# A two-layer transformer block on one core: FFN gate and up products by Strassen's scheme for 18 of 22 feature tiles

## The chip, the cores and the metric

The kernel runs on one core of a Trainium2 chip. The metric is the device time of one execution in microseconds (us). The kernel before the change takes 1743.31 us, the median of 3 runs (1742.58 to 1743.42).

The engines are TensorE (PE; PEld is its weight load), VectorE (DVE), ScalarE (ACT), GpSimd (POOL) and SyncE (SP), which issues every DMA of this kernel. Matrix products are written to PSUM, in banks of 128 x 512 fp32; everything else lies in SBUF. DVE and ACT can read PSUM, POOL works on SBUF only.

## The reference, cut to what matters

```
for l in range(2):
    h = rms_norm(x, g_pre_mix[l])
    mix = hybrid_mixer(h, ...)                      # four attention branches, gates, w_out
    x = x + rms_norm(mix, g_post_mix[l])
    h = rms_norm(x, g_pre_ffn[l])
    f = (silu(h @ w_ffn_gate[l]) * (h @ w_ffn_up[l])) @ w_ffn_down[l]
    x = x + rms_norm(f, g_post_ffn[l])
```

There are 512 tokens, the model is 1024 wide (8 tiles of 128) and the FFN 2816 wide (22 tiles of 128, `FT`). All of it is float32.

## The kernel before, in words

**Three products for one.** A product of float32 matrices is made of three fp32r products. Each operand x is split into hi, a rounded copy made by ACT, and lo = x - hi, made by DVE or POOL. `mm3` (L304) issues hi·hi, hi·lo and lo·hi into one PSUM bank (L306, L307, L308); the lo·lo product is left out. Each of the three has a weight load of its own.

**Layout.** In the FFN, features lie on the partitions and the 512 tokens on the free axis. `u` holds the 8 split tiles of the FFN's input, times its gain but not yet times the rms factor of each token. That factor, broadcast over the partitions, is `rB`.

**Weights.** `plan()` (L58) lists all weight tiles in the order in which they are used; the host lays them out in that order. `w_load` (L231) has SP load a tile of 128 x 1024 (512 KB) into one of three `raw` buffers. `conversion` (L249) splits it into `whi` and `wlo` (four buffers each) in two halves of 512 columns: an ACT cast (L271) and a DVE subtraction (L272) for each half. `take` (L280) hands the next tile out and converts two tiles ahead (`CL`).

**The FFN.** `ffn` (L1385) goes over the 22 feature tiles. `fm` (L772) takes a weight tile and issues 8 x 3 products of 512 columns into a PSUM bank, once for gate and once for up. DVE multiplies the gate product by `rB` (L1390), ACT applies silu (L1391), POOL multiplies by `rB` again (L1392), which stands for the factor of the up product, DVE multiplies by the up product (L1409), and ACT and POOL split the result into hi and lo (L298, L299) for the down product. The first five of the 44 products are issued at the end of `out_block` (L1252), which hands them over as `ps`.

**What follows.** In layer 0, `down_block` (L1162) takes one column of 128 features after the other over 22 feature tiles. In layer 1, `finish` (L1428) has tokens on the partitions and weights 256 columns wide as the moving operand (`tm`, L792 to L794). Both read the residual only near their ends: `x` in layer 0, and in layer 1 `xt`, which `to_tokens` (L1415) makes of `x` by transposes during the FFN.

**Order.** Tile assigns the order of instructions on each engine when the program is built, by dependencies and program order, except between `ordered(True)` and `ordered(False)`, where the order is as written. Each engine then runs its own queue in that order. `act` is a pool of 63 buffers of 128 x 512 (`AB`), tag `a`; `hp` has 12 more for the hidden tiles.

Of the kernel before, what the change touches and what calls it, by code (L numbers as in the profile page):

```python
# [17 lines left out]
S = 512  # L18
# [28 lines left out]

G0, G1, S1, TS, GT = 2, 4, 4, 5, 3
SQ = 3
LAST_K = ((0, 2), (2, 2), (4, 2), (6, 2), (8, 4), (12, 4), (16, 4), (20, 2))  # L50


def _ktiles(w, k0, nk, cols):
    w = w[k0 * 128:(k0 + nk) * 128][:, cols]
    return w.reshape(nk, 128, -1).transpose(1, 0, 2)


def plan():  # L58

    out = []  # L60

    def add(name, nk, nc, f):
        out.append((name, nk, nc, f))

    for l in range(LAYERS):
        def w_in(name, k0, nk, cols):
            add(name, nk, len(cols), lambda a, l=l: _ktiles(a["w_in"][l], k0, nk, cols))

        def rng(key, n, o=0):
            return np.arange(OFF[key] + o, OFF[key] + o + n)  # L70
# [22 lines left out]
        for m in range(FT):  # L93
            for key in ("w_ffn_gate", "w_ffn_up"):
                add(key, 8, 128, lambda a, l=l, m=m, key=key:
                    _ktiles(a[key][l], 0, 8, np.arange(m * 128, m * 128 + 128)))
        if l < LAYERS - 1:
            for d in range(8):
                for k0, nk in ((0, 8), (8, 8), (16, 6)):
                    add("down", nk, 128, lambda a, l=l, d=d, k0=k0, nk=nk:  # L100
                        _ktiles(a["w_ffn_down"][l], k0, nk, np.arange(d * 128, d * 128 + 128)))
        else:
            for c in range(4):
                for k0, nk in ((0, 4), (4, 4), (8, 4), (12, 4), (16, 4), (20, 2)) if c < 3 else LAST_K:
                    add("held" if c == 3 and nk == 2 and k0 < 8 else "downt", nk, 256, lambda a, l=l, c=c, k0=k0, nk=nk:
                        _ktiles(a["w_ffn_down"][l], k0, nk, np.arange(c * 256, c * 256 + 256)))
    return out


# [84 lines left out]
class Builder:  # L194
# [28 lines left out]
    def stream_init(self):  # L223
        self.wi = 0
        self.n_dma = self.n_conv = 0
        self.woff = [0]
        for _, nk, nc, _ in self.plan:
            self.woff.append(self.woff[-1] + 128 * nk * nc)
        self.raw, self.whl = {}, {}

    def w_load(self, upto):  # L231
        while self.n_dma <= min(upto, len(self.plan) - 1):
            i = self.n_dma
            _, nk, nc, _ = self.plan[i]
            n = nk * nc

            t = self.a() if i < 2 else self.wraw.tile([128, 1024], F32, tag="raw", name="raw")
            self.nc.sync.dma_start(
                t[:, :n], self.ap["wts"][self.woff[i]:self.woff[i + 1]].rearrange("(p n) -> p n", p=128))
            self.raw[i] = t  # L240
            self.n_dma += 1

    def w_conv(self, upto):

        while self.n_conv <= min(upto, len(self.plan) - 1):
            for f in self.conversion():
                f()

    def conversion(self, lo_engine=None):  # L249
# [5 lines left out]
        t = self.raw.pop(i)  # L255
        kh = (nk + 1) // 2
        if name == "held":
            tiles = [(self.ar(), self.ar()) for _ in range(2 if nk * ncol > 512 else 1)]
            if len(tiles) == 1:
                kh = nk  # L260
# [19 lines left out]
    def take(self, name, ahead=None):  # L280
        i = self.wi
        assert self.plan[i][0] == name, (self.plan[i][0], name)
        self.w_conv(i + (CL if ahead is None else ahead))
        self.wi += 1
        return self.whl.pop(i)


    def split(self, src, scale=None, lo_engine=None):
# [59 lines left out]
                                  start=True, stop=True)  # L348
        return ss

    def rms(self, ss, nt=4):

        r, steps = self.rms_steps(ss, nt)
        for _ in steps:
            pass
        return r

    def rms_steps(self, ss, nt=4):
        v, r, t = (self.small(nt) for _ in range(3))

        def steps():
            self.nc.vector.tensor_scalar(v, ss[:, 0:nt], 1.0 / D, RMS_EPS, op0=ALU.mult, op1=ALU.add)
            yield
            yield from self.root(v, r, t)
        return r, steps()

# [478 lines left out]
        return acc[0]  # L845

    def next_factors(self, ss):
        self.rT = self.rms(ss)

    def next_spread(self):  # L850
        ps = self.spread(self.rT)
# [310 lines left out]
    def down_block(self, xs, gain, x, next_gain):  # L1162
# [28 lines left out]

        def sums(half):
            ss[half] = self.token_sums(acc, None, 2 * half, 2)
            r[half], chain[half] = self.rms_steps(ss[half], 2)

        def start(half):
            rb[half] = self.spread(r[half], 2)[:, 0:256]
# [184 lines left out]
        self.ordered(False)  # L1382
        return u, y, out

    def ffn(self, l, u, ps):  # L1385
        nc = self.nc
        hid = []

        def silu(z, s, ps, rb):
            nc.vector.tensor_mul(z, ps, rb)  # L1390
            nc.scalar.activation(s, z, AF.Silu)  # L1391
            nc.gpsimd.tensor_mul(s, s, rb)  # L1392

        def keep(s):
            if len(hid) >= FT - 6:
                pr = tuple(self.hp.tile([128, 512], F32R, tag="h", name="h") for _ in range(2))
            else:
                pr = self.ar(), self.ar()
            hid.append(pr)
            return pr  # L1400

        for m in range(FT):
            gate = ps.pop(0) if ps else (yield from self.fm("w_ffn_gate", u))
            z, s = self.a(), self.a()
            silu(z, s, gate, self.rB)
# [3 lines left out]
            nc.vector.tensor_mul(s, s, up)  # L1409
            pr = keep(s)  # L1410
            self.split_to(pr[0], pr[1], s, lo_engine=nc.gpsimd)
            yield 3
        return hid

    def to_tokens(self, x, xt):  # L1415
        nc = self.nc
# [11 lines left out]
    def finish(self, hid, xt):  # L1428
# [8 lines left out]
        for c in range(4):  # L1437
            def evac(t, ps, c=c):
# [6 lines left out]
                if c == 2:  # L1445
                    s1 = before[:, t:t + 1]
                    nc.vector.tensor_reduce(s1, ss[:, 4 * t:4 * t + 3], axis=mybir.AxisListType.X, op=ALU.add)
                    nc.vector.tensor_scalar(s1, s1, 1.0 / D, RMS_EPS, op0=ALU.mult, op1=ALU.add)
# [36 lines left out]
    def build(self):  # L1485
        nc, tc = self.nc, self.tc
        with ExitStack() as ctx:
# [6 lines left out]
            self.ct = cp.tile([128, NCON], F32, name="ct")  # L1494
            self.vt = cp.tile([128, NVEC], F32, name="vt")
            self.gnh = cp.tile([128, 4], F32, name="gnh")
            self.stream_init()
            nc.sync.dma_start(self.vt, self.ap["vec"])
            x = []
# [11 lines left out]
            for l in range(LAYERS):  # L1511
                last = l == LAYERS - 1
                with tc.tile_pool(name="pt%d" % l, bufs=2) as self.ptp:
# [10 lines left out]
                with tc.tile_pool(name="hid%d" % l, bufs=12) as self.hp:  # L1524
                    xt = {}
                    if last:
                        self.bg.append(("xt", self.to_tokens(x, xt)))
                    hid = self.collect(self.ffn(l, u, ps))
                    del u
                    if last:  # L1530
                        self.drain("xt")
                        self.run(self.finish(hid, xt))
# [65 lines left out]
```

## Time and profile before

| | |
|---|---|
| median of 3 runs | 1743.31 us |
| the profiled execution's own time | 1747.27 us |
| its span, first to last instruction | 1745.4 us |
| busy: PE, PEld, DVE, ACT, POOL | 98%, 84%, 52%, 42%, 27% |
| mean granted TensorE clock | 0.994 |
| read from HBM / written | 156.97 MB / 4.19 MB |

All durations below come from the one profiled execution, whose own time is 3.96 us above the median. A matmul's duration in the trace runs from its issue to its end, and matmuls overlap, so the spacing of starts says what one costs in a stream.

### The profile page before, as it was taken

The numbers are of one execution on the slowest core, as the hardware profiler recorded it, in microseconds if no ns is written. First come the engines' busy times: TensorE is split into PE (matmuls) and PEld (weight loads), VectorE is DVE, ScalarE is ACT, GpSimd is POOL, SyncE is SP. The second block draws the span as 40 slices with busy tenths as digits, with TensorE's granted clock in tenths as the row PEclk, the third lists the DMA queues.
The fourth block names the chain that finished last, engine by engine and source line by source line (L and its number), as shares of the span: only waits on it lengthen the run. The fifth ranks groups of instructions, "written<-read, shape, count | busy, mean of one in ns | idle before, by whom it ended". The sixth has DMA issues, their size and how long they took to land.

```text
span 1745.4 us, 24355 instructions
## 1 busy us (share of the span) xinstructions
PE 1711.2 (98%) x9044; PEld 1470.4 (84%) x9044; DVE 915.2 (52%) x1824; ACT 730.1 (42%) x1529; POOL 468.2 (27%) x420
## 2 busy tenths in 40 slices
PE   9899999999999999999998999999999999999998
PEld 7788888888898888888887888888888978888998
DVE  6767777455474333322477578665453743333223
ACT  6565653333454333323356656433234543333221
POOL 1244332211243222200233443322121432222000
PEclk9999999999999999999999999999999999999999
DMA  5544322333413333333245442223334222223321
GB/s 192 144 116 115 97 82 71 102 95 100 157 54 117 98 97 98 94 98 100 64 142 141 119 108 85 91 74 96 102 99 144 85 85 97 97 97 103 95 91 64
DMA packets 62423, 179.01 MB, mean 103 GB/s; under 512 B 8160, under 2 KB 8416, under 8 KB 62304
## 3 DMA queue, kind: packets, MB, share of 16 engines
q1 hardware_dynamic: 62304, 177.45, 33.2%
q8 instruction: 72, 1.18, 0.3%
q14 instruction: 47, 0.39, 0.1%
HBM read 156.97 MB, written 4.19 MB: 92 GB/s over the span
## 4 chain that ended last, share of the span: by engine, by line
PE 84%; DVE 6%; issue 2%; POOL 1%; ACT 1%; DMA 1%; SPq 0%; DVEq 0%; POOLq 0%; ACTq 0%
PE acc L306 21%; PE acc L308 21%; PE acc L307 21%; PE b L523 2%; PE b L443 1%; PE b L469 1%; DVE wlo L272 1%; PE b L794 1%; PE b L793 1%; PE b L792 1%; PE acc L829 1%; PE acc L831 1%; PE acc L830 1%; PE b L1480 1%; PE b L1481 1%
## 5 line engine op out<-in xcount | busy, mean ns | idle before, releaser
L306 PE MATMUL acc<-a,whi 128*128 128x512 f32 (+1 forms) x1760 | 682.4, 388 | 0.0
L308 PE MATMUL acc<-a,wlo 128*128 128x512 f32 (+1 forms) x1760 | 674.9, 384 | 0.0
L307 PE MATMUL acc<-a,whi 128*128 128x512 f32 (+1 forms) x1760 | 674.4, 383 | 0.0
L271 ACT CAST whi<-raw 128x512 fp32r<-128x512 f32 (+3 forms) x586 | 319.0, 587 | 683.1 <-issue 450.9
L272 DVE TENSOR_TENSOR wlo<-raw,whi 128x512 fp32r<-128x512 f32 (+3 forms) x582 | 399.5, 721 | 208.0 <-ACT whi L271 207.1
L308 PEld LDWEIGHTS acc<-a,wlo 128*128 128x128 f32 x1760 | 331.7, 188 | 64.6 <-issue 0.5
L307 PEld LDWEIGHTS acc<-a,whi 128*128 128x128 f32 x1760 | 332.4, 189 | 60.3 <-DVE a L302 0.6
L306 PEld LDWEIGHTS acc<-a,whi 128*128 128x128 f32 x1760 | 332.3, 189 | 59.8 <-issue 1.0
L299 POOL TENSOR_TENSOR a<-a 128x512 fp32r<-128x512 f32 (+1 forms) x80 | 114.9, 1437 | 318.9 <-ACT a L298 313.5
L1092 POOL TENSOR_TENSOR a<-a 128x512 f32<-128x512 f32 x48 | 70.5, 1470 | 247.9 <-DVE a L1091 229.2
L1073 DVE TENSOR_TENSOR a<-acc,a 128x512 f32<-128x512 f32 x64 | 44.2, 691 | 136.6 <-PE acc L308 136.5
L1392 POOL TENSOR_TENSOR a<-a 128x512 f32<-128x512 f32 x44 | 63.5, 1443 | 172.9 <-ACT a L1391 172.9
L1409 DVE TENSOR_TENSOR a<-a,acc 128x512 f32<-128x512 f32 x42 | 28.9, 687 | 139.6 <-PE acc L308 135.3
L1390 DVE TENSOR_TENSOR a<-acc,a 128x512 f32<-128x512 f32 x42 | 29.0, 691 | 134.0 <-PE acc L308 130.6
L462 POOL TENSOR_SCALAR a<-a,sm 128x128 f32<-128x128 f32 (+1 forms) x96 | 59.7, 624 | 90.8 <-DVE sm L461 66.6
L298 ACT CAST a<-a 128x512 fp32r<-128x512 f32 (+1 forms) x86 | 53.2, 618 | 66.9 <-DVE a L631 20.3
L1106 POOL TENSOR_TENSOR a<-a 128x512 f32<-128x512 f32 x26 | 35.0, 1347 | 161.8 <-ACT a L1105 161.2
L454 ACT ACTIVATE a<-a,sm 128x128 f32<-128x128 f32 (+1 forms) x96 | 53.8, 561 | 31.6 <-DVE sm L452 13.3
L480 DVE TENSOR_TENSOR ptl<-b,pth 128x128 fp32r<-128x128 f32 (+1 forms) x96 | 46.5, 486 | 31.3 <-ACT pth L479 30.9
L443 PE MATMUL b<-a 128*128 128x128 f32 (+4 forms) x224 | 51.7, 325 | 4.5 <-DVE a L742 4.4
L829 PE MATMUL acc<-whi,a 128*128 128x256 f32 x192 | 55.6, 290 | 0.0
L831 PE MATMUL acc<-whi,a 128*128 128x256 f32 x192 | 54.4, 283 | 0.0
(258 smaller groups left out, 2475.9 us busy)
## 6 DMA issues: line engine op xcount, KB each, us to landing
raw<-wts SPq DMA_DIRECT2D x242, 512.0 KB, 3.5
a<-a SPq DMA_DIRECT2D x108, 128.0 KB, 2.3
raw<-wts SPq DMA_DIRECT2D x40, 256.0 KB, 2.6
a<-xT SPq DMA_DIRECT2D x16, 256.0 KB, 5.6
raw<-wts SPq DMA_DIRECT2D x7, 452.0 KB, 3.4
a<-tab SPq DMA_DIRECT2D x12, 256.0 KB, 3.9
raw<-wts SPq DMA_DIRECT2D x8, 384.0 KB, 3.1
a<-a SPq DMA_DIRECT2D x32, 64.0 KB, 2.0
```

Of the source, the lines that this page charges most:

```text
L271: todo.append(lambda hi=hi, src=src, n=n: nc.scalar.copy(hi[:, :n], src))
L272: todo.append(lambda hi=hi, lo=lo, src=src, n=n: (lo_engine or nc.vector).tensor_sub(lo[:, :n], src, hi[:, :n].bitcast(F32)))
L299: (lo_engine or nc.vector).tensor_sub(lo, src, hi.bitcast(F32))
L306: mm(out, w[0], x[0], start=start, stop=False)
L307: mm(out, w[0], x[1], start=False, stop=False)
L308: mm(out, w[1], x[0], start=False, stop=stop)
L443: nc.tensor.matmul(ps[:, :L], q[:, qs], k[:, :L], start=j == 0, stop=j == len(qk[h]) - 1)
L462: nc.gpsimd.tensor_scalar(A[:, :L], A[:, :L], rr, 1.0, op0=ALU.mult, op1=ALU.mult)
L829: mm(o, x[0][:, ts], w[0][k % 4], start=k == 0, stop=False)
L831: mm(o, x[1][:, ts], w[0][k % 4], start=False, stop=k == KT - 1)
L1092: nc.gpsimd.tensor_add(merged[dd], merged[dd], t)
L1392: nc.gpsimd.tensor_mul(s, s, rb)
```

## The change

Strassen's scheme (in Winograd's form) multiplies two matrices, each cut into 2 x 2 blocks, with 7 block products in place of 8 and some sums of blocks. Here the blocks of the weights are `a11`, `a12` (input features 0 to 511, feature tiles m and m+1) and `a21`, `a22` (input features 512 to 1023); one block holds gate and up, 128 x 1024 in SBUF. The blocks of the input are features by token halves of 256.

- Feature tiles 0 to 3 (`CM`) stay as they were, save that the second multiplication by `rB` is left out; the FFN's output is then off by a factor per token, which the later rms norm takes out, with its epsilon scaled to match (`eps`).
- Tiles 4 to 21 go in 9 groups of two. A group has seven block products, each of 24 matmuls of 256 columns (2 halves `j`, gate and up, by 4 k by 3). `quarter_steps` makes the seven weight operands: `a11`, p = a21+a22, q = p+a11, v = q+a12, r = a11+a21, `a12`, `a22`, each split as a whole of 1024 columns. p, q and v are POOL additions, r a DVE addition.
- `quarter_operands` makes the seven input operands once per layer: three are halves of `u`, four are sums of halves of the unsplit input (gain times `y`), split.
- The partial results are copied or added out of PSUM after each product (`copy`, `after_v`, ...). Groups alternate between the two PSUM tags.
- The hidden tiles 0 to 13 (`NF`) stay unsplit until the FFN's end, where `split_rest` splits them; tiles 14 to 21 are split at once, as before. The down products take tiles 14 to 21 first (`ORDER`).
- To free 8 `act` buffers, the residual is written to DRAM (`put_away`) and read back after the FFN (`bring_back`). `hp` becomes two 128 x 1024 buffers (`fraw`) for raw weights and eight of 128 x 512 for hidden tiles.

```diff
+CM = 4
+NF = 14
+ORDER = tuple(range(NF, FT)) + tuple(range(NF))
+AHEAD = 2
...
+        for m in range(CM, FT, 2):
+            for k0, i in ((0, 0), (0, 1), (4, 1), (4, 0)):
+                add("quarter", 8, 128, lambda a, l=l, m=m + i, k0=k0: np.concatenate(
+                    [_ktiles(a[key][l], k0, 4, np.arange(m * 128, m * 128 + 128))
+                     for key in ("w_ffn_gate", "w_ffn_up")], axis=1))
...
+    def quarters_ahead(self, n):
+        while self.q_todo and self.q_done <= n + self.q_used:
+            self.q_todo.popleft()()
+            self.q_done += 1
...
+        def plain(src):
+            hi = self.whi.tile([128, 1024], F32R, tag="whi", name="whi")
+            lo = self.wlo.tile([128, 1024], F32R, tag="wlo", name="wlo")
+            nc.scalar.copy(hi, src)
+            nc.vector.tensor_sub(lo, src, hi.bitcast(F32))
+            self.quarter.append((hi, lo))
+        def total(x, y, engine, i):
+            pool, tag = ((self.wlo, "wlo"), (self.whi, "whi"))[i]
+            t = pool.tile([128, 1024], F32, tag=tag, name="sum")
+            engine.tensor_add(t, x, y)
+            return t
+        def one():
+            load(3)
+            st["i"] = self.n_conv
+            st["a11"] = self.raw.pop(self.n_conv)
+            plain(st["a11"])
+        def two():
+            i = st["i"]
+            a21, a22 = st["a21"], st["a22"] = self.raw.pop(i + 1), self.raw.pop(i + 2)
+            st["p"] = total(a21, a22, nc.gpsimd, 0)
+            st["q"] = total(st["p"], st["a11"], nc.gpsimd, 1)
+            plain(st.pop("p"))
+            load(4)
+        def three():
+            st["a12"] = self.raw.pop(st["i"] + 3)
+            st["v"] = total(st["q"], st["a12"], nc.gpsimd, 0)
+            plain(st.pop("q"))
+        def four():
+            st["r"] = total(st.pop("a11"), st.pop("a21"), nc.vector, 1)
+            plain(st.pop("v"))
+            load(5)
...
+    def quarter_operands(self, u, y, gain):
+        f = [self.a() for _ in range(KT)]
+        for k in (0, 4, 1, 5, 2, 6, 3, 7):
+            nc.vector.tensor_scalar_mul(f[k], y[k], gain(k))
...
+        for k in range(4):
+            nc.gpsimd.tensor_sub(put(0, k), f[k][:, h0], f[k][:, h1])
+        for k in range(4):
+            stt(put(1, k), put(0, k), -1.0, f[k + 4][:, h1], op0=ALU.mult, op1=ALU.subtract)
+        split(0)
...
+        return [plain(0, h0), tiles(0), tiles(1), plain(4, h1), tiles(2), plain(4, h0), tiles(3)]
+    def quarter_products(self, ops, tag, done):
+        banks = [(self.ps(tag), self.ps(tag)) for _ in range(2)]
+        for i, x in enumerate(ops):
+            self.quarters_ahead(AHEAD)
+            hi, lo = self.quarter.popleft()
+            self.q_used += 1
+            for j in range(2):
+                chain, other = banks[j]
+                o = (chain[:, 0:256], other[:, 0:256], other[:, 256:512])[(0, 1, 0, 1, 0, 2, 0)[i]]
+                for k in range(4):
...
+                    mm(o, hi[:, c], x[k][0], start=first, stop=False, ...)
+                    mm(o, hi[:, c], x[k][1], start=False, stop=False, ...)
+                    mm(o, lo[:, c], x[k][0], start=False, stop=k == 3, ...)
+                if i in done:
+                    done[i](j, o)
+                yield 6
...
     def ffn(self, l, u, ps, y, xt=None):
         def keep(s):
+            hid.append(s)
+            if len(hid) > NF:
+                hid[-1] = self.split(s, lo_engine=nc.gpsimd)
...
+            def after_r(j, o):
+                nc.scalar.copy(e[3][:, HALF[j]], o)
+                if j == 1:
+                    nc.gpsimd.tensor_add(e[3], e[3], e[1])
+            def after_a12(j, o):
+                d = (z[0], w)[j]
+                nc.vector.tensor_add(d[:, h0], o, e[0][:, HALF[j]])
+                if j == 0:
+                    nc.vector.tensor_mul(z[0], z[0], self.rB)
+                    nc.scalar.activation(z[0], z[0], AF.Silu)
+                    nc.vector.tensor_mul(z[1][:, h1], e[3][:, h0], self.rB[:, h1])
+                else:
+                    nc.vector.tensor_mul(z[0], z[0], w)
+                    keep(z[0])
+            def after_a22(j, o):
+                if j == 0:
+                    nc.vector.tensor_mul(z[1][:, h0], o, self.rB[:, h0])
+                    nc.scalar.activation(z[1], z[1], AF.Silu, scale=-1.0)
+                else:
+                    stt(z[1][:, h1], e[3][:, h1], -1.0, z[1][:, h1], op0=ALU.mult, op1=ALU.mult)
+                    stt(z[1][:, h0], o, -1.0, z[1][:, h0], op0=ALU.mult, op1=ALU.mult)
+                    keep(z[1])
...
+    def put_away(self, x):
+        for k in range(KT):
+            self.nc.sync.dma_start(self.away[k], x[k])
...
+    def split_rest(self, hid):
+        for m in range(NF):
+            hi = self.ar()
+            lo = self.hq.tile([128, 512], F32R, tag="h", name="h") if m > NF - 7 else self.ar()
+            self.split_to(hi, lo, hid[m], lo_engine=(nc.vector, nc.vector, nc.gpsimd)[m % 3])
+            hid[m] = hi, lo
+        return [hid[m] for m in ORDER]
```

## Rows read from the trace of the kernel before

**Rows 1.** The page: span, busy time of each engine, chain that ended last.

```profile
span 1745.4 us, 24355 instructions
...
PE 1711.2 (98%) x9044; PEld 1470.4 (84%) x9044; DVE 915.2 (52%) x1824; ACT 730.1 (42%) x1529; POOL 468.2 (27%) x420
...
PE 84%; DVE 6%; issue 2%; POOL 1%; ACT 1%; DMA 1%; SPq 0%; DVEq 0%; POOLq 0%; ACTq 0%
PE acc L306 21%; PE acc L308 21%; PE acc L307 21%; PE b L523 2%; PE b L443 1%; PE b L469 1%; DVE wlo L272 1%; PE b L794 1%; PE b L793 1%; PE b L792 1%; PE acc L829 1%; PE acc L831 1%; PE acc L830 1%; PE b L1480 1%; PE b L1481 1%
```

**Rows 2.** Windows: FFN of layer 0, of layer 1, then finish; columns by header.

```profile
core 0: us, PE busy (x) PEld busy (x) DVE busy (x) ACT busy (x) POOL busy (x), PEclk, DMA share, GB/s
...
560.00:735.00 175.00, 175.00 (x774) 144.96 (x773) 61.41 (x98) 53.87 (x97) 48.70 (x33) 1.00 0.32 96
1412.00:1602.00 190.00, 190.00 (x840) 157.39 (x839) 65.73 (x105) 58.02 (x105) 52.94 (x35) 1.00 0.29 97
1612.00:1706.00 94.00, 94.00 (x785) 94.00 (x785) 26.64 (x48) 24.63 (x59) 1.56 (x1) 1.00 0.29 90
```

**Rows 3.** Timeline of PE: two starts, 75 matmuls apart; start us, duration us.

```profile
478.92 0.28 PE L306 MATMUL acc<-a,whi 128*128 128x256 f32 x1
...
487.91 0.28 PE L306 MATMUL acc<-a,whi 128*128 128x256 f32 x1
```

**Rows 4.** Groups by line, FFN of layer 0, 560 to 735 us.

```profile
L272 DVE TENSOR_TENSOR wlo<-raw,whi 128x512 fp32r<-128x512 f32 x66 | 42.4, 684 | 0.0
L1390 DVE TENSOR_TENSOR a<-acc,a 128x512 f32<-128x512 f32 x16 | 11.1, 692 | 55.7 <-PE acc L308 55.7
...
L1392 POOL TENSOR_TENSOR a<-a 128x512 f32<-128x512 f32 x16 | 23.4, 1465 | 62.6 <-ACT a L1391 62.6
...
L271 ACT CAST whi<-raw 128x512 fp32r<-128x512 f32 x64 | 36.5, 619 | 120.5 <-issue 116.9 <-PE acc L307 3.6
L1391 ACT ACTIVATE a<-a 128x512 f32<-128x512 f32 x16 | 10.1, 628 | 0.1
```

**Rows 5.** Single lines: durations of one, ns, min/median/max; last row a mean.

```profile
L1392 POOL TENSOR_TENSOR a<-a x44: 1279/1475/1479, 531.6 to 1607.9; 128x512 f32<-128x512 f32 x44
...
L1117 POOL TENSOR_TENSOR a<-a x42: 727/918/1195, 493.4 to 1373.5; 128x256 f32<-128x256 f32 x42
L1117 DVE TENSOR_TENSOR a<-a x6: 417/418/419, 493.3 to 1367.8; 128x256 f32<-128x256 f32 x6
...
L271 ACT CAST whi<-raw 128x256 fp32r<-128x256 f32 x72 | 25.7, 405 | 102.6 <-issue 79.9 <-PE acc L307 15.9 <-PE b L794 6.5
```

**Rows 6.** Timeline of POOL, then of DVE, 543 to 550 us.

```profile
543.29 1.30 POOL L299 TENSOR_TENSOR a<-a 128x512 fp32r<-128x512 f32 x1 [1.45 <-ACT a L298]
544.87 1.42 POOL L1392 TENSOR_TENSOR a<-a 128x512 f32<-128x512 f32 x1 [0.27 <-ACT a L1391]
...
543.77 3.07 DVE L272 TENSOR_TENSOR wlo<-raw,whi 128x512 fp32r<-128x512 f32 x2 [0.49 <-ACT whi L271]
...
548.70 1.29 DVE L272 TENSOR_TENSOR wlo<-raw,whi 128x512 fp32r<-128x512 f32 x2
```

**Rows 7.** Windows around two PE stalls (columns as rows 2), and PE's timeline.

```profile
519.00:521.00 2.00, 1.12 (x11) 0.94 (x9) 1.90 (x4) 0.00 (x0) 0.00 (x0) 1.00 0.00 0
521.00:525.00 4.00, 4.00 (x23) 4.00 (x23) 2.76 (x9) 1.23 (x3) 0.00 (x0) 0.57 0.41 131
916.00:920.00 4.00, 1.82 (x14) 1.54 (x13) 2.60 (x4) 2.23 (x4) 0.34 (x1) 1.00 0.92 362
...
918.99 0.64 PE L676 MATMUL b<-ct,a 128*96 128x128 f32 x4 [2.18 <-DVE a L869]
```

**Rows 8.** DMA issues (KB each, median us to landing), and SP's issues of L238.

```profile
raw<-wts SPq DMA_DIRECT2D x242, 512.0 KB, 3.5
...
kept<-a SPq DMA_DIRECT2D x8, 256.0 KB, 2.2
a<-kept SPq DMA_DIRECT2D x8, 256.0 KB, 5.3
...
L238 SPq DMA_DIRECT2D raw<-wts x297: 327/328/737, 3.5 to 1705.9; - x149
```

More of the change, by code (lines that the diff above doesn't have):

```diff
@@ L92, in plan @@
             add("out", 8, 128, lambda a, l=l, d=d: _ktiles(a["w_out"][l], 0, 8, np.arange(d * 128, d * 128 + 128)))
-        for m in range(FT):
+        for m in range(CM):
             for key in ("w_ffn_gate", "w_ffn_up"):
@@ L235, in w_load @@
             n = nk * nc
-            t = self.a() if i < 2 else self.wraw.tile([128, 1024], F32, tag="raw", name="raw")
+            if i < 2:
+                t = self.a()
+            elif self.plan[i][0] == "quarter" and (i - self.plan_q[i]) % 5 > 2:
+                t = self.hp.tile([128, 1024], F32, tag="fraw", name="raw")
+            else:
+                t = self.wraw.tile([128, 1024], F32, tag="raw", name="raw")
             self.nc.sync.dma_start(
@@ L257, in conversion @@
         if name == "held":
-            tiles = [(self.ar(), self.ar()) for _ in range(2 if nk * ncol > 512 else 1)]
-            if len(tiles) == 1:
-                kh = nk
+            kh = nk
+            if self.n_held < 2:
+                t2 = self.hp.tile([128, 1024], F32R, tag="fraw", name="held")
+                tiles = [(t2[:, 0:512], t2[:, 512:1024])]
+            else:
+                tiles = [(self.ar(), self.ar())]
+            self.n_held += 1
         else:
@@ new lines, in quarter_steps, with load, five, six @@
+    def quarter_steps(self):
+        nc = self.nc
+        st = {}
+        def load(n):
+            self.w_load(self.n_conv + n)
+        def plain(src):
[29 more added lines that the diff above has]
+            load(5)
+        def five():
+            plain(st.pop("r"))
+        def six():
+            plain(st.pop("a12"))
+            load(6)
+        def seven():
+            plain(st.pop("a22"))
+            self.n_conv += 4
+            self.q_end = self.n_conv
+        return [one, two, three, four, five, six, seven]
@@ new lines, in quarter_products @@
+    def quarter_products(self, ops, tag, done):
+        mm = self.nc.tensor.matmul
+        banks = [(self.ps(tag), self.ps(tag)) for _ in range(2)]
[6 more added lines that the diff above has]
+                o = (chain[:, 0:256], other[:, 0:256], other[:, 256:512])[(0, 1, 0, 1, 0, 2, 0)[i]]
+                for k in range(4):
+                    c = slice(512 * j + 128 * k, 512 * j + 128 * k + 128)
+                    first = i in (0, 1, 5) and k == 0
+                    mm(o, hi[:, c], x[k][0], start=first, stop=False, skip_group_check=i in (2, 3, 4, 6))
+                    mm(o, hi[:, c], x[k][1], start=False, stop=False, skip_group_check=i in (2, 3, 4, 6))
+                    mm(o, lo[:, c], x[k][0], start=False, stop=k == 3, skip_group_check=i in (2, 3, 4, 6))
+                if i in done:
+                    done[i](j, o)
+                yield 6
@@ L1383, in out_block, with ffn, whole @@
         return u, y, out
-    def ffn(self, l, u, ps):
+    def ffn(self, l, u, ps, y, xt=None):
         nc = self.nc
         hid = []
[L1389 to L1392, printed above, removed]
         def keep(s):
[L1395 to L1402, printed above, removed]
-            gate = ps.pop(0) if ps else (yield from self.fm("w_ffn_gate", u))
-            z, s = self.a(), self.a()
-            silu(z, s, gate, self.rB)
+            hid.append(s)
+            if len(hid) > NF:
+                hid[-1] = self.split(s, lo_engine=nc.gpsimd)
+        def whole(m):
+            return self.hq.tile([128, 512], F32, tag="h", name="h") if m < 8 else self.a()
+        ops = None
+        self.quarters_init()
+        for m in range(CM):
+            gate = ps.pop(0) if ps else (yield from self.fm("w_ffn_gate", u))
+            z = whole(m)
+            nc.vector.tensor_mul(z, gate, self.rB)
+            nc.scalar.activation(z, z, AF.Silu)
+            if not ps and ops is None:
+                ops = self.quarter_operands(u, y, lambda k: self.vec("pre_ffn", 8 * l + k))
+                if xt is None:
+                    self.put_away(y)
             if not ps:
@@ L1408, in ffn @@
             up = ps.pop(0) if ps else (yield from self.fm("w_ffn_up", u, "b" if m == 2 else "acc"))
-            nc.vector.tensor_mul(s, s, up)
-            pr = keep(s)
-            self.split_to(pr[0], pr[1], s, lo_engine=nc.gpsimd)
+            nc.vector.tensor_mul(z, z, up)
+            keep(z)
             yield 3
-        return hid
+        if xt is not None:
+            self.drain("xt")
+            self.put_away([xt[t, h] for t in range(4) for h in range(2)])
+            xt.clear()
+        del y
```

98 lines of the change are left out of this document (83 added, 15 removed).

## The prediction

> **What bounds the kernel now.** I read the page first, for its busy shares and for the chain that ended last [rows 1]: PE is busy 98% of the span and 84% of the chain, led by the three lines of `mm3`. A busy PE need not be PE at its peak, so the stage is read next. In the FFN's two stretches [rows 2] PE has no gap and the granted clock is 1.00, the level of 2.4 GHz, while DVE is busy 61.4 of 175 us, ACT 53.9 and POOL 48.7. So the FFN lasts as long as its matmuls, and the price of one is their spacing: 774 in 175 us, 226.1 ns, for 512 columns. For 256 columns there are two places: `finish`, 785 in 94 us, 119.7 ns [rows 2], and the half columns of `out_block`, with weights stationary as in the new code, where 75 matmuls take 487.91 - 478.92 = 8.99 us, 119.9 ns [rows 3]. A half-width matmul thus costs 53% of a full one, its own weight load included.
>
> **The products.** A pair of feature tiles has 2 x 2 x 24 = 96 matmuls of 512 columns, 96 x 226.1 = 21.71 us. It gets 7 x 24 = 168 of 256, 168 x 119.7 = 20.12 us; one block product lasts 2.87 us. The gain is 1.59 us a group, and 28.6 us over the 18 groups of both layers, if nothing else comes late. Saving an eighth of the columns gives only 7.3%, since narrow matmuls cost more by the column.
>
> The Trainium skill (TensorE: Matmul & The Clock Gate, Back-to-back issue gap) gives the spacing as N/2.4 + 2.5 ns, 215.8 and 109.2 ns. By that the group would gain 20.72 - 18.35 = 2.37 us and the kernel an estimated 42.7 us. The trace differs (226.1 and 119.7), so that sum isn't used.
>
> **What makes the operands.** The question is whether the operands come in time, and DVE and POOL decide that together. At 543 us POOL works on two instructions and DVE has two subtractions of SBUF tiles to do [rows 6]. They take 3.07 us, where two take 1.29 us undisturbed, and they end only 0.55 us after POOL's second instruction does (544.87 + 1.42 = 546.29; 543.77 + 3.07 = 546.84). POOL's 1.42 us is in turn above its least of 1.28 [rows 5]. So these do not overlap: their times add. DVE's operations with one input in PSUM do not show this (L1390: mean 692 ns, with POOL at work in the same stretch [rows 4]). ACT is free of it.
>
> Now the new instructions. None of 1024 columns is in the trace. POOL's least times for 256 and 512 columns are 0.727 and 1.279 us [rows 5], so a sum of 1024 is about 1.279 + 2 x 0.552 = 2.38 us (twice 1.279 = 2.56 at most). DVE takes 0.418 and about 0.69 us for 256 and 512 [rows 4, 5], 0.64 in a stream of 512, thus 0.64 + 2 x 0.27 = 1.19 us for 1024 (1.28 at most). I take the lower values, since each instruction's start cost is paid once. ACT by the same slope takes 0.619 + 2 x 0.214 = 1.05 us.
> - Per group, POOL: p, q, v and the sum in `after_r`, 3 x 2.38 + 1.28 = 8.42 us.
> - Per group, DVE on SBUF alone: seven subtractions and r, 8 x 1.19 = 9.52 us, and in the evacuation two of 512 and two of 256 columns, 2 x 0.64 + 2 x 0.37 = 2.02 us.
> - Sum 19.96 us, against 20.12 us of PE. DVE's six PSUM operations (2.2 us) may lie beside POOL.
> - From the sixth group on, the two hidden tiles are also split, with POOL subtractions: 2 x 1.28, sum 22.5 us.
> - ACT: seven casts, 7.35 us, six half copies of about 0.4 and two silus of 0.63, 11.0 us. It has room.
>
> Before, a pair asked the shared resource for 4 x 1.28 + 8 x 0.64 = 10.2 of 21.7 us. So the cover of the new work is nearly used up, and four groups in nine want more than a group lasts.
>
> **Where it lands.** With four `whi` and four `wlo` buffers and `AHEAD` 2, a step's operand can be made only when the product three places before it has ended, so some two product times, 5.7 us, are left for it. After a group's fifth product the work is densest: the sum in `after_r` 1.28, p 2.38, three evacuations 1.65, lo of p 1.19, q 2.38, an evacuation 0.37, v 2.38, lo of q, r, lo of v 3.57, 15.2 us, due in five products, 14.4 us. Afterwards four subtractions are left for some 6 us and the lag is made up. So:
> - Entering groups 2 to 6: PE waits 0 to 0.8 us each, as p may start earlier; taken 0.3, five times 1.5 us.
> - Entering groups 7 to 9, behind splits of 2.56 us: 15.2 + 2.56 - 14.4 = 3.4 us late, or 1.0 if p goes 2.4 us ahead. Between them I take 2.0, 6.0 us in all. The upper end is 4.7 each, with a loss of clock: in one stall PE sat idle under 1 us before and after a few tiny products, and then the granted clock was 0.57 from 521 to 525, where 23 matmuls took 4.0 us instead of 2.75, 1.25 us lost; after another, of 2.18 us, it stayed at 1.00 [rows 7].
> - The input operands, once a layer: 8 DVE multiplications (0.64, the row of 512 columns being the nearest, though it has two inputs), 8 POOL differences of 256 (0.73), 8 DVE of 256 (0.37), 8 subtractions of 512 (0.64), 19.0 us; three weight tiles still to convert, 3.8 us; lo of `a11`, p and lo of p, 4.8 us: 27.6 us. They are due when the second product starts, after `up` of tile 2, tile 3 and one product, 3 x 24 x 0.2261 + 2.87 = 19.1 us. Late by 8.5 us if all goes first, 0 if only the first sum is made first (9.7 us of the 19.0 can wait) and its multiplications start ahead of `rB`. Taken 3 us.
> - `split_rest`: ten DVE and four POOL subtractions, 11.5 us, and 14 ACT casts, 8.7 us. In layer 0 the first eight tiles cover 8 x 3 x 0.226 = 5.4 us and the rest are wanted one each 0.68 us, while no next group asks for operands: 0 to 4 us, taken 1. In layer 1 the first eight tiles of `tm` last 4 x 8 x 3 x 0.1197 = 11.5 us, so 0 (0 to 2).
> - Residual: 16 more transfers of 256 KB a layer; one takes 2.2 us out and 5.3 us in [rows 8], and SP 0.33 us to issue, so 2.6 us for eight. Nobody waits for the residual until the down products end, tens of us later. On SP the group's weight loads, 3.5 us each, queue behind the writes; five raw buffers cover them. Without cover, 2.1 MB at the 362 GB/s of [rows 7] is 5.8 us once a layer; taken 0.
> - Removed: POOL's product at L1392, the split of 14 tiles during the FFN, two-part conversion; none was waited for by PE. The added epsilon product is one small DVE operation, 0.
>
> **Sum.** Stalls are 2 x (1.5 + 6.0 + 3) + 1 = 22.0 us. The net is 28.6 - 22.0 = 6.6 us faster. The profiled execution took 1747.27 us, so 1740.7; it stands 3.96 us above the median of 1743.31, and there the time is **1736.7**, written as 1737. A measurement of this kernel can tell about 0.2% (3.5 us) from no change.
>
> **Rivals.**
> - *All is hidden* (0.17). POOL's sums start ahead, the input operands fit into DVE's idle time before `rB`, the splits wait their turn. For it: DVE and POOL are each busy under 36% now. Against: the sum of 19.96 in 20.12. It gives 28.6 down to 16 us, 1714.7 to 1727.
> - *The gain is just eaten* (0.16): stalls between 25 and 32 us, 1740 to 1747.
> - *DVE and POOL become the bound* (0.26). If hand-overs leave 5% of their common time unused, a group lasts 19.96/0.95 = 21.0 us, and 22.5/0.95 = 23.7 us with splits: 5 x 0.9 + 3 x 3.6 = 15.3 us of stalls a layer, with 5 at the start and 1.5 at the end 21.8, twice that less 28.6 is 15 us slower, 1758; lost clock adds some us. It decides from 14.3 us of stalls a layer. For it: [rows 6], and a chain p, q, v in which POOL's work can't be brought forward at will. Against: the static order can move POOL's sums one product ahead, and the lag of one group is made up within it. The Trainium skill (SBUF — State Buffer, SBUF: two separate sides) calls the port pair that DVE and GpSimd share an exclusive lock held for a whole instruction. The trace agrees (3.07 for 1.29 us).
> - *The narrow products cost more here* (0.03): the change pays only under 21.71/168 = 129 ns a matmul. Both streams show under 120. At 135 ns it is 1743.31 + 18 x 0.97, 1761.
>
> **How the numbers follow.** My forecast, half to nine tenths of the gain eaten, 1727 to 1740, has 0.38. Faster is 0.38 + 0.17 = 0.55, same 0.16, slower 0.26 + 0.03 = 0.29. The range 1719 to 1762 leaves out the best third or so of the first rival and the far side of the third and fourth, under 2 in 10; the likeliest case's own is 1727 to 1740.
>
> **What would show it.** Right: 1512 matmuls a layer of 256 columns spaced 120 ns inside products; POOL sums near 2.4 us, DVE subtractions of 1024 near 1.2 us and longer when POOL runs; PE idle at the entry to the group products and more before groups 7 to 9 than before 2 to 6, released by DVE's lo; DVE and POOL together some 95% of a group. Wrong: PE without gaps (first rival), every group above 21.7 us (third), or gaps that end on ACT, on raw loads or on a free `act` buffer, which this sum has at nothing.

## The result, and the profile after

| | before | after |
|---|---|---|
| median, 4 runs each | 1743.37 us | 1790.1 us (1787.66 to 1791.56) |
| ratio to before, 95% interval | | 1.0265 (1.0247 to 1.0282) |
| profiled execution / its span | 1747.27 / 1745.4 us | 1791.56 / 1789.8 us |
| mean granted TensorE clock | 0.994 | 0.981 |

The change makes the kernel 2.65% slower, some 46 us, outside the range that was forecast. In the experiments below, one execution of the kernel before (1875.47 us) and one of the third experiment's kernel (4248.89 us) lie far outside the others, and the ratios leave them out. The page of after first; [rows 1] has the same lines of before.

```profile
span 1789.8 us, 27392 instructions
...
PE 1707.2 (95%) x10340; PEld 1525.6 (85%) x10340; DVE 1153.9 (64%) x2004; ACT 829.9 (46%) x1671; POOL 561.8 (31%) x444
...
PE 44%; DVE 8%; issue 2%; ACT 1%; POOL 1%; DMA 0%; SPq 0%; DVEq 0%; ACTq 0%; POOLq 0%
...
L451 PE MATMUL acc<-a,whi 128*128 128x256 f32 x560 | 163.6, 292 | 15.4 <-ACT a L1605 15.1
...
L351 DVE TENSOR_TENSOR wlo<-sum,whi 128x1024 fp32r<-128x1024 f32 x72 | 125.9, 1748 | 7.8 <-ACT whi L350 6.1
...
L358 POOL TENSOR_TENSOR sum<-sum,raw 128x1024 f32<-128x1024 f32 x36 | 92.7, 2575 | 64.5 <-issue 47.1
```

PE is busy for nearly as long as before (1707.2 against 1711.2 us), but now it also stands idle, 82.6 us in all (1789.8 - 1707.2) where it was 34.2. Ahead of its matmuls of L451 into `acc` it stood idle 15.1 us until an operation of ACT, L1605, had ended. DVE's subtraction of 1024 columns takes 1748 ns in the mean, where its shortest takes 1210. The windows of the group products, columns as in [rows 2], say where:

```profile
547.00:686.00 139.00, 129.81 (x1051) 126.92 (x1050) 110.13 (x116) 67.25 (x108) 57.81 (x25) 1.00 0.28 92
686.00:761.00 75.00, 63.42 (x459) 62.40 (x458) 56.29 (x55) 34.95 (x58) 30.89 (x16) 0.86 0.24 79
1443.00:1581.00 138.00, 130.72 (x1061) 128.22 (x1060) 104.35 (x108) 65.46 (x104) 57.23 (x25) 1.00 0.28 92
1581.00:1656.00 75.00, 63.41 (x461) 62.40 (x460) 56.47 (x56) 35.16 (x58) 30.40 (x16) 0.86 0.27 83
```

The first and third rows are groups 1 to 6 and the start of 7, the others the rest. PE had no gap in [rows 2]; here 9.2 of 139 us are idle, and behind the splits 11.6 of 75 us, at a granted clock of 0.86. DVE and POOL together are busy 167.9 us of the first 139, so for 28.9 us at least both stand in an instruction at once. Their timelines over the end of one group show that an instruction can stand there without running (start us, duration us; DVE, then POOL, then the waits of PE):

```profile
634.45 2.61 DVE L1623 TENSOR_TENSOR a<-a 128x256 f32<-128x256 f32 x1 [3.54 <-POOL a L1614]
636.99 0.41 DVE L1619 TENSOR_TENSOR a<-b,a 128x256 f32<-128x256 f32 x1
...
638.37 1.22 DVE L351 TENSOR_TENSOR wlo<-sum,whi 128x1024 fp32r<-128x1024 f32 x1
...
640.44 3.10 DVE L351 TENSOR_TENSOR wlo<-sum,whi 128x1024 fp32r<-128x1024 f32 x1
...
630.22 2.95 POOL L358 TENSOR_TENSOR sum<-raw 128x1024 f32<-128x1024 f32 x1 [9.93 <-PE b L453]
633.12 1.29 POOL L1614 TENSOR_TENSOR a<-a 128x512 f32<-128x512 f32 x1
634.37 2.41 POOL L358 TENSOR_TENSOR sum<-sum,raw 128x1024 f32<-128x1024 f32 x1
639.72 2.74 POOL L358 TENSOR_TENSOR sum<-sum,raw 128x1024 f32<-128x1024 f32 x1 [2.94 <-issue]
...
617.47 0.39 PE L453 MATMUL b<-a,wlo 128*128 128x256 f32 x1 [0.62 <-DVE wlo L351]
621.42 0.39 PE L453 MATMUL b<-a,wlo 128*128 128x256 f32 x1 [0.81 <-DVE wlo L351]
639.64 0.39 PE L453 MATMUL acc<-a,wlo 128*128 128x256 f32 x1 [0.64 <-DVE wlo L351]
```

DVE's L1623 has 256 columns and takes 2.61 us. It starts 0.08 us after POOL's q (634.37) and ends 0.28 us after q does (637.06 against 636.78). It had waited 3.54 us before, for POOL's sum of `after_r` (L1614), which stood in POOL's queue behind p. So the low part of p comes only at 638.37, though p was ready at 633.17, and PE waits for it in the second product of the next group at 639.64. The low part of q (640.44) then meets v on POOL and takes 3.10 us, and PE waits again in the third product. That happens at the entry of nearly every group up to the sixth: the first wait recurs after 22.17 us (617.47 and 639.64), where the matmuls need 20.12 and the old pair took 21.71.

Behind the splits it is a longer wait. The same views of the entry of group 7, for DVE, POOL, ACT and PE:

```profile
684.78 3.09 DVE L351 TENSOR_TENSOR wlo<-sum,whi 128x1024 fp32r<-128x1024 f32 x1
687.80 1.48 DVE L1633 SCALAR_TENSOR_TENSOR a<-a 128x256 f32<-128x256 f32 x1
689.20 0.41 DVE L1634 SCALAR_TENSOR_TENSOR a<-b,a 128x256 f32<-128x256 f32 x1
...
684.06 2.73 POOL L358 TENSOR_TENSOR sum<-sum,raw 128x1024 f32<-128x1024 f32 x1 [2.94 <-issue]
686.75 2.24 POOL L470 TENSOR_TENSOR a<-a 128x512 fp32r<-128x512 f32 x1
...
689.70 0.62 ACT L469 CAST a<-a 128x512 fp32r<-128x512 f32 x1 [1.83 <-DVE a L1634]
690.22 0.92 ACT L1605 COPY a<-acc 128x256 f32<-128x256 f32 x3
...
690.64 0.58 PE L451 MATMUL acc<-a,whi 128*128 128x256 f32 x1 [3.76 <-ACT a L1605]
```

The third product writes the PSUM bank of the first, and may not before ACT has copied it out (L1605). The copy stands in ACT's queue behind the cast of a finished hidden tile (L469), the cast waits for DVE's L1634, and that stands on DVE behind two instructions that POOL's v and POOL's split L470 hold up: 3.09 us for 1.22, 1.48 for 0.41. PE waits 3.76 us. When it starts again the granted clock has fallen to the level of 1.2 GHz, as two windows show:

```profile
690.60:697.00 6.40, 6.36 (x34) 6.36 (x35) 4.82 (x4) 4.06 (x8) 1.29 (x1) 0.59 0.46 166
...
690.64:695.00 4.36, 4.36 (x20) 4.36 (x21) 3.56 (x3) 2.76 (x6) 1.25 (x1) 0.50 0.66 238
```

34 matmuls take 6.4 us instead of 34 x 0.1197 = 4.1, until the clock is back at 1.00 at about 696 us. The wait for L1605 occurs six times, three in a layer, 22.6 us, and from one to the next (690.64, 717.51, 744.57) it is 26.9 and 27.1 us.

**The account.** The nine groups last 214.7 us in layer 0 and 211.8 in layer 1, where nine pairs took 9 x 21.71 = 195.4: 19.3 + 16.4 us more. In layer 1 PE waits once more, 6.71 us at the transposes of the hand-over to tokens (1.4 us in all in before), because DVE's L1589, which frees the PSUM bank they want, stood behind four operations of the input operands (L424) that took 6.25 us together, beside POOL's differences and sums:

```profile
1424.90 6.25 DVE L424 SCALAR_TENSOR_TENSOR a<-a 128x256 f32<-128x256 f32 x4
...
1432.42 1.12 PE L1669 MATMUL b<-ct,a 128*128 128x128 f32 x4 [6.71 <-DVE h L1589]
```

The start of the down products in layer 0 loses some 4.0 us: three waits of 3.2 us together, and a wider spacing of the matmuls behind them, at a granted clock of 1.00. Together 19.3 + 16.4 + 5.3 + 4.0 = 45.0 us; the two spans differ by 44.4.

### The profile page after: what moved, and what is told of

The parts are those of the page before. It is cut to its first block, busy times and chain, and to the rows that moved or that the text cites. A ratio compares the mean times of both kernels' runs of the same rounds, so it can differ in the third digit from the quotient of the medians.

```text
span 1789.8 us, 27392 instructions
## 1 busy us (share of the span) xinstructions
PE 1707.2 (95%) x10340; PEld 1525.6 (85%) x10340; DVE 1153.9 (64%) x2004; ACT 829.9 (46%) x1671; POOL 561.8 (31%) x444
## 4 chain that ended last, share of the span: by engine, by line
PE 44%; DVE 8%; issue 2%; ACT 1%; POOL 1%; DMA 0%; SPq 0%; DVEq 0%; ACTq 0%; POOLq 0%
PE acc L477 8%; PE acc L478 8%; PE acc L479 8%; PE acc L453 2%; PE acc L451 2%; PE acc L452 1%; DVE wlo L351 1%; PE b L971 1%; PE b L970 1%; PE b L969 1%; PE b L453 1%; PE b L451 1%; PE b L452 1%; PE b L700 1%; DVE wlo L303 1%
## 5 line engine op out<-in xcount | busy, mean ns | idle before, releaser
L477 PE MATMUL acc<-a,whi 128*128 128x512 f32 (+1 forms) x1238 | 479.3, 387 | 0.0
L479 PE MATMUL acc<-a,wlo 128*128 128x512 f32 (+1 forms) x1238 | 471.2, 381 | 0.0
L478 PE MATMUL acc<-a,whi 128*128 128x512 f32 (+1 forms) x1184 | 451.5, 381 | 3.3 <-DVE a L470 2.8
L477 PEld LDWEIGHTS acc<-a,whi 128*128 128x128 f32 x1238 | 234.9, 190 | 39.4 <-issue 1.0
L478 PEld LDWEIGHTS acc<-a,whi 128*128 128x128 f32 x1184 | 224.6, 190 | 43.0 <-DVE a L470 4.2
L451 PE MATMUL acc<-a,whi 128*128 128x256 f32 x560 | 163.6, 292 | 15.4 <-ACT a L1605 15.1
L453 PE MATMUL acc<-a,wlo 128*128 128x256 f32 x560 | 164.3, 293 | 8.7 <-DVE wlo L351 8.5
L470 POOL TENSOR_TENSOR a<-a 128x512 fp32r<-128x512 f32 (+1 forms) x64 | 94.5, 1477 | 226.2 <-ACT a L469 222.9
L452 PE MATMUL acc<-a,whi 128*128 128x256 f32 x560 | 162.8, 291 | 0.0
L1269 POOL TENSOR_TENSOR a<-a 128x512 f32<-128x512 f32 x48 | 70.4, 1469 | 248.0 <-DVE a L1268 229.1
L453 PE MATMUL b<-a,wlo 128*128 128x256 f32 x448 | 130.7, 292 | 7.9 <-DVE wlo L351 7.6
L451 PE MATMUL b<-a,whi 128*128 128x256 f32 x448 | 129.4, 289 | 7.5 <-ACT a L1605 7.5
L351 DVE TENSOR_TENSOR wlo<-sum,whi 128x1024 fp32r<-128x1024 f32 x72 | 125.9, 1748 | 7.8 <-ACT whi L350 6.1
L452 PE MATMUL b<-a,whi 128*128 128x256 f32 x448 | 128.9, 288 | 0.0
L451 PEld LDWEIGHTS acc<-a,whi 128*128 128x128 f32 x560 | 112.1, 200 | 16.5 <-ACT a L1605 15.9
L453 PEld LDWEIGHTS acc<-a,wlo 128*128 128x128 f32 x560 | 111.9, 200 | 11.6 <-DVE wlo L351 11.6
L358 POOL TENSOR_TENSOR sum<-sum,raw 128x1024 f32<-128x1024 f32 x36 | 92.7, 2575 | 64.5 <-issue 47.1
```

The costliest lines, as they stand in the source:

```text
L351: nc.vector.tensor_sub(lo, src, hi.bitcast(F32))
L358: engine.tensor_add(t, x, y)
L451: mm(o, hi[:, c], x[k][0], start=first, stop=False, skip_group_check=i in (2, 3, 4, 6))
L452: mm(o, hi[:, c], x[k][1], start=False, stop=False, skip_group_check=i in (2, 3, 4, 6))
L453: mm(o, lo[:, c], x[k][0], start=False, stop=k == 3, skip_group_check=i in (2, 3, 4, 6))
L470: (lo_engine or nc.vector).tensor_sub(lo, src, hi.bitcast(F32))
```

## The experiments

The theory (called the lock): POOL's operations and DVE's operations on two SBUF tiles exclude each other, and in DVE's queue the short evacuations (the operations that take results out of PSUM) stand behind those that are held up. The rival: the order of the queues alone does it, as with ACT's copy behind the cast (called the queue), whatever engine makes the sums.

**The split deferred.** The hidden tiles are split after the fourth product of the next group, so no cast stands ahead of the copies.

```diff
-                hid[-1] = self.split(s, lo_engine=nc.gpsimd)
+                pending.append(len(hid) - 1)
...
             def after_v(j, o):
...
+                if j == 1:
+                    split_pending()
```

> The changed kernel with one thing moved: the hidden tiles of a group are split after the fourth product of the next group and not at once. Queue theory (ACT's copy of the first product out of PSUM stands in ACT's queue behind the cast of a hidden tile that is late, and TensorE may not write that bank before): the six waits of 3.8 us on L1605 go, groups 7 to 9 fall from 26.9 to about 22.2 us, total about 1790 - 28 = 1762 us. Lock theory (DVE and POOL together have 22.5 us of work in these groups, whatever the order): they stay at 22.5 to 23.7 us, 1766 to 1771 us, and the waits reappear on DVE's lo.

Measured: 1774.65 us, ratio 1.0168 (1.0142 to 1.0193). The waits for L1605 are gone, 22.6 us of idle time, but by the ratios only 17 us came back. Group 7 falls to 22.2 us, as the queue theory expected of all three; groups 8 and 9 take 24.7 and 24.4, with a wait for the low part at their entry:

```profile
708.34 0.38 PE L453 MATMUL b<-a,wlo 128*128 128x256 f32 x1 [2.83 <-DVE wlo L351]
```

So the order of ACT's queue carried the lateness to PE in one form; without it the lateness arrives in another. Both theories expected a faster kernel than this one.

**The three sums p, q and v on DVE.** Nothing else changes.

```diff
-            st["p"] = total(a21, a22, nc.gpsimd, 0)
-            st["q"] = total(st["p"], st["a11"], nc.gpsimd, 1)
+            st["p"] = total(a21, a22, nc.vector, 0)
+            st["q"] = total(st["p"], st["a11"], nc.vector, 1)
...
-            st["v"] = total(st["q"], st["a12"], nc.gpsimd, 0)
+            st["v"] = total(st["q"], st["a12"], nc.vector, 0)
```

> The changed kernel with the weight sums p, q and v on DVE and not on POOL, the splits where they were. Lock theory (DVE's subtractions stand still while POOL's sums of 2.4 us run): the waits of 0.6 and 0.8 us for lo at the second and third product go, a group without splits falls from 22.2 to about 20.4 us, the waits of 3.8 us get shorter by the 1.9 us that lo of q waited for v, total about 1757 us. Rival (DVE is simply loaded to its limit, and gets 3.6 us more a group): the waits stay or grow, 1785 us or more.

Measured: 1726.66 us, ratio 0.9897 (0.9874 to 0.9919). More work on the busier engine, and 63 us less than after. The page has it in one line:

```profile
PE 1681.6 (98%) x10340; PEld 1506.8 (87%) x10340; DVE 1141.1 (66%) x2058; ACT 832.5 (48%) x1671; POOL 438.1 (25%) x390
```

DVE makes 54 sums more (2058 instructions against 2004) and is busy 12.8 us less (1141.1 against 1153.9), so its busy time in after held more than work. The queue theory falls: ACT's cast still stands ahead of the copies, and PE's longest wait for L1605 is 0.9 us. The change gave back more than the lock theory had expected, since that had shortened the waits for ACT by only 1.9 us each; nearly all of them went. This run alone can't tell the lock from sums that merely come late from POOL; the fifth and eighth were made for that.

**Both together.** The two edits above in one kernel.

> Both of the above: late splits, and sums on DVE. If queue and lock theory both hold, all groups last about 20.4 us, and 12 x 1.8 + 6 x 6.5 = 60 us go, total about 1730 us, below the kernel before. If DVE's load takes over, groups stay near 21.5 us and the total is 1750 us or more.

Measured: 1730.12 us, ratio 0.9911 (0.9886 to 0.9937). That is the time expected if both theories hold, but the second experiment reaches it alone: with the sums on DVE, the deferral adds nothing.

**The residual alone.** The kernel before, with the residual written to DRAM ahead of the FFN and read back after it.

```diff
+                    if not last:
+                        self.put_away(x)
                     hid = self.collect(self.ffn(l, u, ps))
...
+                        self.put_away([xt[t, h] for t in range(4) for h in range(2)])
...
+                    x = self.bring_back()
```

> The kernel before, with one part of the change alone: the residual is written to DRAM at the FFN's start (layer 1: at its end) and read back before the down products. The prediction had it at nothing: the same time as before within 0.2%. If the transfers delay weight loads it is up to 12 us slower (2 x 5.8).

Measured: 1744.56 us, ratio 1.0002 (0.9989 to 1.0015). No cost shows, within 0.15%.

**POOL made busy again, first form.** The sums stay on DVE; per group ten POOL additions of 256 columns into a scratch buffer that nobody reads.

```diff
+        def again(x, n):
+            for i in range(n):
+                nc.gpsimd.tensor_add(self.junk, x[:, 128 * i:128 * i + 256], x[:, 512:768])
...
+            again(a22, 6)
...
+            again(st["a12"], 4)
```

> The kernel with p, q and v on DVE (e2_dve_sums), and POOL does ten additions of 256 columns more a group, on the same raw weights and at the same places, into a scratch tile that nobody reads: about 7.3 us of POOL, as the three sums took there (7.2 us). No operand waits for them. Lock theory: DVE's subtractions stand still behind them all the same, and DVE has 3.6 us more than in the changed kernel, so the waits come back: 22 us a group or more, 1760 us or above. Rival (the sums on POOL were merely slow and late as data: 2.4 us and not 1.2, three in a chain): the scratch work is hidden, 1727 us as in e2_dve_sums.

Measured: 1829.22 us, ratio 1.0486 (1.0469 to 1.0504). The loss is back, and larger, but it doesn't tell the two apart: the sum of `after_r` still ran on POOL, stood there behind the scratch additions, and DVE waited for it. The eighth experiment repeats this without that link.

**The input operands and the last splits on DVE too.**

```diff
-            nc.gpsimd.tensor_sub(put(0, k), f[k][:, h0], f[k][:, h1])
+            nc.vector.tensor_sub(put(0, k), f[k][:, h0], f[k][:, h1])
...
-            nc.gpsimd.tensor_sub(put(2, k), f[k + 4][:, h1], f[k][:, h1])
+            nc.vector.tensor_sub(put(2, k), f[k + 4][:, h1], f[k][:, h1])
...
-            self.split_to(hi, lo, hid[m], lo_engine=(nc.vector, nc.vector, nc.gpsimd)[m % 3])
+            self.split_to(hi, lo, hid[m], lo_engine=nc.vector)
```

> The kernel with p, q and v on DVE (e2_dve_sums), and on DVE too the differences for the input operands and all of split_rest's subtractions; POOL keeps the sum after r and the lo of the hidden tiles. Lock theory: the waits at the start of the down products in layer 0 (3.4 us, four DVE subtractions took 5.6 us beside POOL's) and of the transposes in layer 1 (2.4 us) go or halve, so 3 to 6 us less, about 1722 us. If DVE's load decides, it is the same or slower, 1727 us or more.

Measured: 1719.14 us, ratio 0.9853 (0.9839 to 0.9868), about 7.5 us less where 3 to 6 were expected. The wait of the transposes in layer 1 is gone.

**The sum of `after_r` on DVE as well.** Now POOL has next to nothing to do during the groups.

```diff
-                    nc.gpsimd.tensor_add(e[3], e[3], e[1])
+                    nc.vector.tensor_add(e[3], e[3], e[1])
```

> e6_rest_dve with the sum after r on DVE as well (0.64 us in place of POOL's 1.28), so that POOL has nothing left in the group products but the lo of the last hidden tiles. PE has no wait left there, so both theories expect no change: 1719 us within 3 us. It is the base of the next run.

Measured: 1712.74 us, ratio 0.9812 (0.9798 to 0.9827), 6 us better than expected and the fastest kernel of this case, 33 us under before on the same chip. Both theories had expected no change. Groups 7 to 9 of both layers still took 20.3 to 20.7 us in the sixth experiment and take 20.16 here, which is 2.5 us of it; the rest was not followed. The window of layer 0's groups, and DVE's timeline at a group's end:

```profile
546.00:728.00 182.00, 182.00 (x1516) 181.88 (x1515) 163.53 (x204) 103.12 (x166) 9.30 (x7) 1.00 0.29 102
```

```profile
622.82 0.68 DVE L1614 TENSOR_TENSOR a<-a 128x512 f32<-128x512 f32 x1
623.42 0.42 DVE L1619 TENSOR_TENSOR a<-b,a 128x256 f32<-128x256 f32 x1
623.76 0.41 DVE L1623 TENSOR_TENSOR a<-a 128x256 f32<-128x256 f32 x1
...
625.03 1.21 DVE L358 TENSOR_TENSOR sum<-sum,raw 128x1024 f32<-128x1024 f32 x1
...
626.76 1.22 DVE L351 TENSOR_TENSOR wlo<-sum,whi 128x1024 fp32r<-128x1024 f32 x1
...
630.03 1.21 DVE L351 TENSOR_TENSOR wlo<-sum,whi 128x1024 fp32r<-128x1024 f32 x1
```

PE has no gap at a clock of 1.00, and the groups last 181.5 us (546.56 to 728.04), nine times 20.16. DVE, with nearly all the work of both engines, is busy 163.53 of 182 us, and its rows above show no held instruction: L1623 takes 0.41 us, the low parts 1.22. Only beside POOL's last seven subtractions (L470) do six of its sums take 1.98 to 2.32 us, and PE waits for none of them.

**POOL made busy, DVE not waiting for it.** The last kernel with the scratch additions of the fifth experiment (same edit). Behind POOL's additions stand only the low parts of the last hidden tiles, which the down products read; nothing in the groups waits for them.

> e7_all_dve, and POOL does the ten additions of 256 columns a group (7.3 us) into a scratch tile that nobody reads. In e5_pool_again DVE also waited 6.7 us for the sum after r, which stood behind them in POOL's queue; here DVE waits for no result of POOL. Lock theory: DVE has 9.5 + 3.6 + 2.0 + 0.6 = 15.7 us a group on SBUF alone, with 7.3 us of POOL 23.0 us, above PE's 20.1: PE waits for lo again, 18 x 2 to 3 us, 1755 to 1775 us. Rival (e5's waits came from POOL's queue alone): the scratch work is hidden, 1719 to 1725 us.

Measured: 1770.57 us, ratio 1.0138 (1.0120 to 1.0156), 58 us more than without the additions. DVE, POOL and the waits of PE (us in total, times, longest):

```profile
630.81 1.76 DVE L358 TENSOR_TENSOR sum<-raw 128x1024 f32<-128x1024 f32 x1
632.49 1.22 DVE L1620 TENSOR_TENSOR a<-a 128x512 f32<-128x512 f32 x1
633.64 0.41 DVE L1625 TENSOR_TENSOR a<-b,a 128x256 f32<-128x256 f32 x1
...
634.39 1.22 DVE L1627 TENSOR_TENSOR a<-a 128x512 f32<-128x512 f32 x1
...
627.38 13.34 POOL L363 TENSOR_TENSOR junk<-raw 128x256 f32<-128x256 f32 x10 [7.63 <-DMA raw<-wts]
```

```profile
PE acc L459 <- DVE wlo L351: 14.8, 16, 1.9
PE b L459 <- DVE wlo L351: 11.4, 13, 1.9
```

DVE's operations on two SBUF tiles go from 0.68 to 1.22 us and from 1.22 to 1.76; L1625, with one input in PSUM, stays at 0.41. POOL's ten additions take 13.34 us where ten at the least time of [rows 5] would take 7.3. Nobody waits for their results. They do keep raw buffers longer, but in layer 0's groups DVE waited only for ACT's casts and once for PE (0.42 us), and in neither layer did DVE or ACT wait for a weight load, so a dependence isn't the cause. This shows the lock. The Trainium skill (SBUF — State Buffer, SBUF: two separate sides) says that a DVE operation with two SBUF inputs and a POOL operation that reads SBUF take a common port pair in turn, each for its whole instruction; the PSUM row and the lengthened ones agree.

**After, with only the sum of `after_r` on DVE.** p, q and v stay on POOL.

```diff
-                    nc.gpsimd.tensor_add(e[3], e[3], e[1])
+                    nc.vector.tensor_add(e[3], e[3], e[1])
```

> The changed kernel with only the sum after r moved from POOL to DVE; p, q, v and the splits stay on POOL. Queue theory (DVE stands idle 3.5 us a group for that sum, because POOL does p first, and this alone makes lo of p and q late): the waits at the second and third product go, about 12 x 1.8 = 22 us less, 1768 us. Lock theory: DVE no longer idles, but its short operations and lo of q still stand behind q and v (2.2 and 1.9 us), so about half goes, 1775 to 1785 us.

Measured: 1790.79 us, ratio 1.0250 (1.0233 to 1.0268), no different from after; both theories expected a gain.

```profile
631.60 2.89 DVE L1614 TENSOR_TENSOR a<-a 128x512 f32<-128x512 f32 x1
634.53 2.51 DVE L1623 TENSOR_TENSOR a<-a 128x256 f32<-128x256 f32 x1
...
641.21 3.36 DVE L351 TENSOR_TENSOR wlo<-sum,whi 128x1024 fp32r<-128x1024 f32 x1
```

DVE no longer waits for POOL's result, but its own sum now meets p on POOL (631.00 to 633.94) and takes 2.89 us in place of 0.68. The time is the same, put down as busy instead of idle.

## Why the prediction was wrong

**The gain** was right: 28.6 us forecast. Without stalls the seventh experiment's groups last 20.16 us each against 20.12; layer 0's nine account for 195.4 - 181.5 = 13.9. The kernel is 33 us faster by its ratio (30 to 35). Of the 34.0 us between the two profiled spans, 14.2 lie between the last factors ahead of layer 0's FFN and the end of its down products, 16.1 between the same place in layer 1 and the end, and 3.8 in stages that the change leaves alone. Why those are shorter was not followed.

**The durations** were right: POOL's sums of 1024 columns take at least 2.39 us (2.38 forecast), DVE's 1.21 to 1.22 (1.19), ACT's casts 1.05 (1.05). So was the reading of [rows 6], that the times of the two engines add. The residual cost nothing, as taken. The stalls stand where forecast, short ones at the entry to groups 2 to 6 and longer ones before 7 to 9.

**The step that failed** is the size of the stalls in "Where it lands". "Entering groups 2 to 6 ... taken 0.3" measured 22.17 - 20.12 = 2.05 us, above even its bound of 0.8. "Entering groups 7 to 9 ... I take 2.0" measured 26.9 - 20.1 = 6.8, above the bound of 4.7: 3.76 us of wait, 2.3 of lower clock in the 6.4 us behind it, the rest mostly in wider spacing of the matmuls next to the waits. Per layer the first three stall terms were taken at 10.5 us; layer 0's groups lost 214.7 - 9 x 20.12 = 33.6, layer 1's 30.7. Three reasons:
- The working added up the shared time of a whole group, 19.96 us of 20.12, and let it be filled without loss and in any order. But DVE works its queue in order. An evacuation of 0.41 us behind a held subtraction waits as long as POOL's sum runs, and everything behind it too. What counted was the chain of the few operations between the fourth product and the next group's second, and there each of p, q and v held up DVE: p because the sum of `after_r`, for which DVE waited, stood behind it in POOL's queue, q and v by the lock. Without the first, the lock takes its place at p (ninth experiment). The seventh and eighth experiments show the lock from both sides.
- The third product's wait on the PSUM bank of the first had no term at all. In ACT's queue the copy stands behind a cast that depends on DVE, and this turned a lateness of DVE into a wait of 3.76 us. The prediction named gaps that end on ACT as something "this sum has at nothing".
- Layer 1's transposes, 6.71 us, had no term either: the DVE operation that frees their bank was queued behind the input operands. These were costed only by when the second product needs them (3 us taken; the first group of layer 0 lasted 2.6 us over 20.12, that of layer 1 nothing), not by what stands behind them on DVE.

Two readings of the working were off without deciding the outcome. A group has eight half copies on ACT, not six: those of `after_r` are missing. And of the 23 matmuls between 521 and 525 us in [rows 7] five have a single column, so the 1.25 us of lost clock was too little: 18 x 0.1197 leaves up to 1.85 us. Even so the bound would be 5.3 us, under the 6.8 measured.

**The end of layer 0**, 1 us taken, lost about 4.0 against before, its bound of 4.

**The rivals.** What happened is the third, DVE and POOL as the bound, with 0.26; 16 of the 18 groups last longer than the 21.7 us named as its sign. Its mechanism is right, its price too low, 1758, for the same reason: it put 5% on the shared time, where hand-overs in a fixed order cost 2 us in 20 and, with ACT's queue, 7. The first rival, that all is hidden, is what the change gives once the sums leave POOL: 1712.74 us there, just under its 1714.7.

## What to carry to other kernels

In this kernel, work given to POOL beside a DVE that works on two SBUF tiles wasn't extra capacity: it took DVE's time at POOL's price, 2.4 us for a sum that DVE makes in 1.2, and all of it on DVE was faster than shared. When two engines take turns, don't sum their busy times over a stage; write down the order of each queue from the event that frees an operand to the matmul that wants it, and ask what each short operation stands behind. A PSUM bank that is used again two products later needs a row of its own in that list, with what is queued ahead of its copy.

## What the hardware showed that was not expected

- The turn-taking holds up POOL as well. An addition of 256 columns, 0.73 us at least in [rows 5], took 3.06 us at 534.00 us in after's input operands, while DVE ran a row of operations on SBUF tiles, and the ten scratch additions took 13.34 us for 7.3.
- In a busy share, time spent held up looks like work: after's 3.54 us of idle DVE ahead of L1623 became, in the ninth experiment, 2.89 us of L1614, 2.2 more than it takes alone, and the time didn't change.
- DVE's scalar-tensor-tensor operation on two SBUF tiles (L1633) is held as well, 1.48 us for 0.41. The same operation with an input in PSUM (L1634) is not: in the second experiment it took 0.42 us at 690.55 us with POOL in its subtractions (688.49 to 694.03), and DVE's next operation on two SBUF tiles took 1.99 us for 1.22.
